# Moving the additions of squared sums from GpSimd to VectorE in a state-space mixer

## The chip, the cores and the metric

The kernel runs on one core of a Trainium2 chip. The metric is the device time of one execution in microseconds (us). The core has a matrix engine (TensorE, PE in the rows; its weight loads are PEld), a vector engine (VectorE, DVE), an engine for functions (ScalarE, ACT), a general one (GpSimd, POOL) and a queue engine (SyncE, SP). Each engine takes its instructions in the order of its own queue and waits on semaphores of the others.

## The reference, cut to what matters

Two layers process 512 prompt positions and 8 samples together. Layer 0 mixes by sparse attention, layer 1 by a state-space (Mamba-2) mixer; each is followed by an MLP. Two norms matter here: the one on the mixer's inner output `y`, and the one on the residual stream ahead of the MLP of layer 1.

```python
def rmsnorm(x, w):
    xf = x.astype(jnp.float32)
    r = lax.rsqrt(jnp.mean(xf * xf, axis=-1, keepdims=True) + EPS)
    return (xf * r).astype(x.dtype) * w
...
def ssd_mixer(h, conv_buf, ssm_state, w_in, conv_w, conv_b, dt_bias, a_log, d_skip, norm_w, w_out):
...
    y = y.astype(h.dtype).reshape(B, T, SSD_D_INNER)
    y = rmsnorm(y * jax.nn.silu(z), norm_w)
    new_state = final.reshape(B, SSD_HEADS, SSD_HEAD_DIM, SSD_STATE).astype(ssm_state.dtype)
    return y @ w_out, new_conv, new_state
...
        xp = xp + mp[2] * op
        xs = xs + ms[2] * os_
        hp = modulate(xp, norm_w[i, 1], mp[3], mp[4])
        hs = modulate(xs, norm_w[i, 1], ms[3], ms[4])
```

## The kernel before, in words

Activations lie with channels on the 128 partitions and the 520 positions (512 prompt, 8 sample) along the free axis. The residual stream is `X`, 8 such tiles; the mixer's inner output is 16 tiles, numbered q. A norm needs the sum of squares over channels: each tile is squared on ACT, the squares of the tiles are added into one tile, and a product with a column of ones on PE sums over the partitions (`rnorm`). A norm can take several tiles, `parts`, one product after the other.

In the state-space stage a loop over q runs `ssd_x` (input product and convolution), `ssd_pair` (two heads: matrices `M`, states `st`, sample states `ss` with `xb`, and `xd` for the products) and `ssd_gate`. `ssd_gate` multiplies `y` by its gate, squares it on ACT into `z`, adds `z` to `yss` at line 1604 on POOL for q of 1 to 14 (q 0 makes `yss`, q 15 is kept in `ysq`), and splits the scaled `y` into a high and a low half, `yh`, on ACT and DVE. All weights are split in the same way (`wh`, ACT line 330 and DVE line 336), since each product is made of three in reduced precision.

After the last tile the output product runs in four groups. In the last, `ssd_out(3, ...)`, each of 8 residual tiles n is finished by `out_add` (line 1631, reads PSUM) and `out_fin` (line 1633): scale `acc`, add to `X` (`c` in the rows), the sample part through a small `t`, then `square` and `scaled` (`us`, and a copy on ACT). `square` gets POOL as its engine there, so that tiles 1 to 6 are added to `ssq` at line 534 on POOL; tile 7 goes to `parts`. In this stage `ssq` lies in a buffer of `st`, and the squares in the two buffers of `M`, which is how the rows call them. `boundary` then makes the norm: products on `st` (that is, `ssq`) and on `M` (tile 7), root, reciprocal, and the modulated input of the MLP. Before it and between, PE has a small product for the conditioning (`ada`).

Elsewhere (`start`, `nsa_out`, `mlp`, `last`) `square` is called without an engine and adds on DVE at line 336.

The order of each queue isn't the order of the code: a scheduler lays the instructions out by priority and planned times, and then sets the semaphores. Buffers of a name rotate; an instruction that writes one waits for the last reader.

Of the kernel before, what the change touches and what calls it, by code (L numbers as in the profile page):

```python
# [14 lines left out]
ALU = mybir.AluOpType  # L15
# [190 lines left out]
BOTH = (0, 1)  # L206


def cols(hs=BOTH):
    return slice(PART[hs[0]][0], PART[hs[-1]][1])  # L210


def prompt(ap, hs=BOTH):
    return two(ap[:, 0:512])[:, hs[0]:hs[-1] + 1]
# [6 lines left out]
def span(ps):  # L221

    return ps.rearrange("p h n -> p (h n)")[:, HP:HP + T]
# [38 lines left out]
class Step:  # L262
# [252 lines left out]
        w = self.nw[:, 2 * l + which, :]  # L515
        self.stt(self.a, self.m[l][:, o + 8:o + 16, :], 1.0, w[:, :, None].to_broadcast([128, 8, 9]), ALU.add, ALU.mult)

    def square(self, k, eng=None, hs=BOTH):
        at = cols(hs)
        x = self.X[:, k, at]  # L520
        if k == 0:
            self.ssq = self.U('ssq')
            self.parts = [self.ssq]
            self.act(self.ssq[:, at], x, AF.Square)

            self.act(self.small([128, 1], 'warm', 2), self.ssq[:, 0:1], AF.Sqrt)
        else:
            s = self.U('sq')
            q = self.ssq[:, at]
            self.act(s[:, at], x, AF.Square)  # L530
            if not eng:
                self.tt(q, q, s[:, at], ALU.add)
            elif k < 7:
                eng.tensor_tensor(self.ssq, self.ssq, s, op=ALU.add)
            else:
                self.parts.append(s)

    def scaled(self, k):
        x = self.X[:, k, :]
# [1049 lines left out]
    def ssd_gate(self, g, t, y):  # L1589

        q = 4 * g + t
        ps = self.product(('w_ssd', 10 * g + 3 + 2 * t), self.h)
        z = self.U('z')
        v = span(ps)
        self.act(z, v, AF.Tanh, scale=0.5)
        self.stt(z, z, 1.0, v, ALU.add, ALU.mult)
        self.tt(y, y, z, ALU.mult)
        if q == 0:
            self.yss = self.U('yss')
            self.act(self.yss, y, AF.Square)  # L1600
        else:
            self.act(z, y, AF.Square)
            if q < 15:
                self.nc.gpsimd.tensor_tensor(self.yss, self.yss, z, op=ALU.add)
            else:
                self.ysq = z
        hi, lo = self.U('yh', F32R), self.U('yh', F32R)
        w = self.snw[:, q:q + 1]
        self.act(hi, y, AF.Copy, scale=w)
        self.stt(lo, y, w, hi, ALU.mult, ALU.subtract)  # L1610
        self.yh[q] = (hi, lo)
# [21 lines left out]
    def out_fin(self, n):  # L1633
        a = self.acc.pop(n)
        self.tt(a, a, self.ry, ALU.mult)
        g = self.m[1][:, 16 + n, :]
        x = self.X[:, n, :]
        self.stt(prompt(x), prompt(a), g[:, 0:1], prompt(x), ALU.mult, ALU.add)
        t = self.small([128, 8], 't8')
        self.tt(t, a[:, 512:T], g[:, 1:9], ALU.mult)  # L1640
        self.tt(x[:, 512:T], x[:, 512:T], t, ALU.add)
        self.square(n, self.nc.gpsimd)
        self.scaled(n)

    def ssd(self, h):
# [326 lines left out]
```

## Time and profile before

| What | us |
|---|---|
| Median of 3 runs | 1719.15 |
| Lowest and highest | 1718.74, 1723.88 |
| Profiled execution | 1717.8 |
| Its span, first to last instruction | 1716.0 |
| PE busy | 1658.1 |
| DVE busy | 983.5 |
| ACT busy | 761.8 |
| POOL busy | 146.4 |

Times in the rows count from the start of the span. A row of a group gives line, engine, operation, names as out<-in, shape and count, then busy time and mean ns of one, then the idle time ahead of it and what ended it. A row of the order of time gives start and duration in us, engine, line, operation and names; in brackets stands the idle time just before. The end of one instruction can lie a little after the start of the next on the same engine.

### The profile page before, as it was taken

The page shows a single profiled execution, that of the slowest core. Times are in us where ns is not written, and L with a number is a line of the kernel's source. Part 1 is how long each engine was busy: PE and PEld are TensorE (multiplying, and loading weights), DVE is VectorE, ACT ScalarE, POOL GpSimd, SP SyncE. Part 2 cuts the span into 40 slices and gives each one's busy share as a digit, 9 for nine tenths or more (in the row PEclk, how much of TensorE's full clock was granted, in tenths as well). Part 3 has the DMA queues.
Part 4 walks back from the last instruction along what each step waited for, and adds up shares of the span by engine and source line. Part 5 has one row for each costly group of instructions (what it writes and reads, how often), then busy time and mean ns, then how long its engine had stood idle before and what let it go on. Part 6 is the DMA issues. An engine that isn't in the chain of part 4 may idle for free.

```text
span 1716.0 us, 34647 instructions
## 1 busy us (share of the span) xinstructions
PE 1658.1 (97%) x13846; PEld 1542.4 (90%) x13846; DVE 983.5 (57%) x2422; ACT 761.8 (44%) x1624; POOL 146.4 (9%) x304
## 2 busy tenths in 40 slices
PE   7999999999999999999999999999998999999997
PEld 6799867667989999999989998999997999999997
DVE  2543377776464343433469968879797643434344
ACT  3534366666443132322456666646564422323231
POOL 1000113310001000000001112111022000000000
PEclk9999999999999999999999999999999999999999
DMA  8823656545433534234433352343324232323221
GB/s 300 290 87 98 215 193 227 166 150 198 135 115 108 175 96 136 88 136 136 137 133 113 132 171 86 119 137 135 129 89 160 75 98 87 99 87 97 88 87 51
DMA packets 72114, 229.87 MB, mean 134 GB/s; under 512 B 8770, under 2 KB 15218, under 8 KB 71186
## 3 DMA queue, kind: packets, MB, share of 16 engines
q1 hardware_dynamic: 62546, 198.45, 35.2%
q0 software_dynamic: 8832, 28.16, 4.6%
q8 instruction: 109, 1.79, 0.4%
q10 hardware_dynamic: 576, 1.05, 0.2%
q14 instruction: 51, 0.42, 0.1%
HBM read 204.02 MB, written 23.61 MB: 133 GB/s over the span
## 4 chain that ended last, share of the span: by engine, by line
PE 69%; DVE 7%; ACT 2%; issue 2%; SPq 1%; POOLq 1%; DMA 0%; POOL 0%; DVEq 0%; ACTq 0%
PE a L323 59%; PE s L323 4%; PE f L323 2%; PE o L323 1%; DVE wh L336 1%; PE sc L323 1%; PE t L327 1%; DVE c L345 1%; ACT wh L330 1%; DVE g L345 1%; PE s L327 1%; DVE acc L336 1%; DVE ss L1465 0%; SPq L395 0%; SPq L393 0%
## 5 line engine op out<-in xcount | busy, mean ns | idle before, releaser
L323 PE MATMUL a<-h,wh 128*128 128x256 f32 x5952 | 743.3, 284 | 4.5 <-ACT t L333 1.6
L323 PEld LDWEIGHTS a<-h,wh 128*128 128x128 f32 x5952 | 723.6, 189 | 10.9 <-issue 3.3
L330 ACT ACTIVATE wh<-w 128x1024 fp32r<-128x1024 f32 x212 | 224.6, 1059 | 522.2 <-PE a L323 479.1
L336 DVE TENSOR_TENSOR wh<-w,wh 128x1024 fp32r<-128x1024 f32 x212 | 259.6, 1225 | 269.4 <-ACT wh L330 268.8
L323 PEld LDWEIGHTS a<-hid,wh 128*128 128x128 f32 x3072 | 370.2, 188 | 5.0 <-issue 4.2
L323 PE MATMUL a<-hid,wh 128*128 128x256 f32 (+1 forms) x3072 | 373.6, 283 | 0.0
L336 DVE TENSOR_TENSOR t<-a,c 128x8 f32<-128x8 f32 x72 | 12.0, 167 | 216.1 <-PE a L323 216.1
L323 PE MATMUL a<-yh,wh 128*128 128x256 f32 (+1 forms) x768 | 99.7, 288 | 3.4 <-DVE acc L336 1.9
L323 PEld LDWEIGHTS a<-yh,wh 128*128 128x128 f32 x768 | 95.0, 191 | 5.6 <-DVE acc L336 2.6
L330 ACT ACTIVATE hid<-t 128x520 fp32r<-128x520 f32 x64 | 40.8, 639 | 84.5 <-DVE t L336 84.5
L330 ACT ACTIVATE h<-t 128x128 f32<-128x128 f32 (+3 forms) x128 | 52.8, 441 | 51.5 <-PE t L327 50.8
L333 ACT ACTIVATE h<-sc,m 128x128 f32<-128x128 f32 (+3 forms) x128 | 66.6, 529 | 10.4 <-DVE m L340 7.4
L336 DVE TENSOR_TENSOR hid<-t,hid 128x520 fp32r<-128x520 f32 x64 | 44.7, 700 | 42.3 <-ACT hid L330 42.3
L345 DVE SCALAR_TENSOR_TENSOR c<-a,c,c 128x512 f32<-128x512 f32 (+1 forms) x74 | 53.9, 728 | 1.8 <-PE a L323 1.8
L327 PE MATMUL t<-c,h 128*128 128x128 f32 x320 | 53.7, 281 | 1.1 <-DVE h L340 0.7
L333 ACT ACTIVATE xb<-bc,x 128x128 f32<-128x128 f32 x128 | 46.4, 419 | 15.6 <-DVE xb L345 11.1
L327 PEld LDWEIGHTS t<-c,h 128*128 128x128 f32 x320 | 35.1, 141 | 14.0 <-issue 8.8
L323 PEld LDWEIGHTS a<-q,wh 128*128 128x128 f32 x384 | 46.3, 188 | 1.0 <-ACT wh L330 0.8
L323 PE MATMUL sc<-kv,q 128*128 128x128 f32 (+3 forms) x128 | 47.1, 380 | 0.0
L323 PE MATMUL a<-q,wh 128*128 128x256 f32 (+1 forms) x384 | 46.7, 283 | 0.0
L323 PE MATMUL sc<-kv,c 128*128 128x128 f32 (+3 forms) x128 | 41.8, 338 | 4.3 <-POOL c L947 4.3
L1465 DVE SCALAR_TENSOR_TENSOR ss<-ss,c,xb 128x128 f32<-128x128 f32 x128 | 43.5, 363 | 3.9 <-ACT xb L333 3.6
(367 smaller groups left out, 1935.9 us busy)
## 6 DMA issues: line engine op xcount, KB each, us to landing
w<-in_w_dram SPq DMA_DIRECT2D x128, 512.0 KB, 3.5
w<-in_ada_w_dram SPq DMA_DIRECT2D x80, 512.0 KB, 3.6
w<-in_w_ssd_dram SPq DMA_DIRECT2D x40, 512.0 KB, 3.6
w<-in_w_nsa_dram SPq DMA_DIRECT2D x20, 512.0 KB, 3.8
ss<-in_ssm_dram SPq DMA_DIRECT2D x16, 512.0 KB, 4.3
out_ssm_s_dram<-ss POOLq DMA_DIRECT2D x16, 512.0 KB, 3.2
w<-in_w_sout_dram SPq DMA_DIRECT2D x16, 512.0 KB, 3.8
cm<-in_cmp_dram SPq DMA_DIRECT2D x24, 256.0 KB, 5.1
```

The lines of the kernel that those rows point to most:

```text
L323: self.nc.tensor.matmul(out, lhsT, rhs, start=start, stop=stop, skip_group_check=True)
L327: self.nc.tensor.transpose(out, in_, self.C('ident')[0:k, 0:k])
L330: self.nc.scalar.activation(out, in_, AF.Copy, **kw)
L333: self.nc.scalar.activation(out, in_, f, **kw)
L336: self.nc.vector.tensor_tensor(out, a, b, op=op)
L345: self.nc.vector.scalar_tensor_tensor(out, a, s, b, op0=op0, op1=op1, **kw)
L1465: self.nc.vector.scalar_tensor_tensor(out, a, s, b, op0=op0, op1=op1)
```

## The change

`square` loses its parameter for an engine and gets `apart`: a tile's squares either go to `parts` or are added on DVE. `out_fin` asks for `apart` at tile 7 alone. In `ssd_gate` the addition to `yss` is made on DVE.

```diff
-    def square(self, k, eng=None, hs=BOTH):
+    def square(self, k, apart=False, hs=BOTH):
...
             self.act(s[:, at], x, AF.Square)
-            if not eng:
+            if apart:
+                self.parts.append(s)
+            else:
                 self.tt(q, q, s[:, at], ALU.add)
-            elif k < 7:
-                eng.tensor_tensor(self.ssq, self.ssq, s, op=ALU.add)
-            else:
-                self.parts.append(s)
...
             self.act(z, y, AF.Square)
             if q < 15:
-                self.nc.gpsimd.tensor_tensor(self.yss, self.yss, z, op=ALU.add)
+                self.tt(self.yss, self.yss, z, ALU.add)
             else:
                 self.ysq = z
...
-        self.square(n, self.nc.gpsimd)
+        self.square(n, n == 7)
         self.scaled(n)
```

## Rows read from the trace of the kernel before

**Rows 1.** The page, first part: busy us (share of the span) and instructions
```profile
PE 1658.1 (97%) x13846; PEld 1542.4 (90%) x13846; DVE 983.5 (57%) x2422; ACT 761.8 (44%) x1624; POOL 146.4 (9%) x304
```
**Rows 2.** Stretches: length, busy PE, PEld, DVE, ACT, POOL, clock, DMA share, GB/s
```profile
930.00:1300.00 370.00, 362.18 (x2955) 343.78 (x2954) 309.23 (x874) 226.45 (x582) 58.60 (x99) 1.00 0.39 130
...
1318.00:1325.00 7.00, 2.73 (x19) 0.60 (x11) 6.93 (x16) 2.99 (x5) 3.42 (x2) 1.00 0.90 328
1325.00:1334.00 9.00, 7.79 (x38) 6.89 (x37) 3.96 (x10) 3.92 (x8) 0.00 (x0) 0.62 0.23 84
...
484.00:490.00 6.00, 6.00 (x30) 5.84 (x31) 6.00 (x15) 3.60 (x10) 0.00 (x0) 0.56 0.10 40
```
**Rows 3.** Who PE waited for, 930 to 1350: us in total, times, longest
```profile
PE s L323 <- DVE xd L336: 3.9, 5, 0.8
PE s L323 <- POOL st L534: 3.9, 1, 3.9
```
**Rows 4.** Groups of instructions on POOL
```profile
L1604 POOL TENSOR_TENSOR yss<-yss,z 128x520 f32<-128x520 f32 x14 | 18.7, 1335 | 90.7 <-ACT z L333 90.7
...
L534 POOL TENSOR_TENSOR st<-st,M 128x520 f32<-128x520 f32 x6 | 9.0, 1494 | 27.3 <-ACT M L333 27.3
```
**Rows 5.** POOL, ACT and PE in order of time, an earlier boundary and this one
```profile
479.35 1.28 PE L323 MATMUL t<-c,ssq 128*128 128x1 f32 x10 [0.60 <-DVE ssq L336]
...
1322.99 1.71 POOL L534 TENSOR_TENSOR st<-st,M 128x520 f32<-128x520 f32 x1 [1.58 <-ACT M L333]
1324.75 1.65 PE L323 MATMUL s<-c,st 128*128 128x1 f32 x10 [3.86 <-POOL st L534]
1325.02 0.64 ACT L333 ACTIVATE M<-c 128x520 f32<-128x520 f32 x1 [1.07 <-DVE c L336]
1326.25 2.27 PE L323 MATMUL s<-c,M 128*128 128x1 f32 x10
```
**Rows 6.** DVE in order of time at the boundary: start, us, instruction
```profile
1305.22 1.81 DVE L345 SCALAR_TENSOR_TENSOR c<-acc,c,c 128x512 f32<-128x512 f32 x1
...
1308.86 1.27 DVE L336 TENSOR_TENSOR us<-c,A 128x8 f32<-128x8 f32 x1
1310.05 0.74 DVE L345 SCALAR_TENSOR_TENSOR c<-acc,c,c 128x512 f32<-128x512 f32 x1
...
1310.79 0.68 DVE L336 TENSOR_TENSOR acc<-acc,a 128x520 f32<-128x520 f32 x1
1311.40 0.15 DVE L336 TENSOR_TENSOR c<-c,t 128x8 f32<-128x8 f32 x1
...
1312.81 1.49 DVE L345 SCALAR_TENSOR_TENSOR c<-acc,c,c 128x512 f32<-128x512 f32 x1
...
1323.47 1.25 DVE L336 TENSOR_TENSOR t<-acc,c 128x8 f32<-128x8 f32 x1
```
**Rows 7.** Groups on DVE by form, 440 to 500, the attention's output stage
```profile
L336 DVE TENSOR_TENSOR ssq<-ssq,sq 128x520 f32<-128x520 f32 x7 | 4.9, 696 | 0.6 <-ACT sq L333 0.6
```
**Rows 8.** DVE in order of time beside additions of `yss` on POOL
```profile
951.44 1.80 DVE L345 SCALAR_TENSOR_TENSOR x<-cv,c,x 128x512 f32<-128x512 f32 x1
...
1049.24 0.61 DVE L1465 SCALAR_TENSOR_TENSOR ss<-ss,c,xb 128x128 f32<-128x128 f32 x2
1049.76 0.29 DVE L345 SCALAR_TENSOR_TENSOR xb<-ss,bc 128x128 f32<-128x128 f32 x1
...
1049.97 1.40 DVE L345 SCALAR_TENSOR_TENSOR xb<-ss,bc 128x128 f32<-128x128 f32 x1
...
1098.50 1.30 DVE L345 SCALAR_TENSOR_TENSOR yh<-y,c,yh 128x520 fp32r<-128x520 f32 x1 [1.33 <-ACT yh L333]
...
1173.90 1.48 DVE L1465 SCALAR_TENSOR_TENSOR ss<-ss,c,xb 128x128 f32<-128x128 f32 x2
...
1278.79 1.58 DVE L1465 SCALAR_TENSOR_TENSOR ss<-ss,c,xb 128x128 f32<-128x128 f32 x2
```
**Rows 9.** The chain that ended last, 1170 to 1182: start, us, what
```profile
1173.98 1.40 DVE ss L1465 x2
```

## The prediction

> **What bounds the kernel now.** I read the page's first part, then the stretches by engine, then who waited for whom, and last the order of time on single engines. The page gives TensorE 97% of the span, VectorE (DVE) 57%, GpSimd (POOL) 9% [rows 1]. That average hides two stages. In the state-space stage, 930 to 1300 us, PE is busy 362.18 of 370 us and DVE 309.23 [rows 2]: PE sets the pace, and DVE, at 84%, is late here and there. At the boundary after it, 1318 to 1325 us, PE is busy only 2.73 of 7 us while DVE is busy 6.93 [rows 2]: there DVE sets the time. The waits agree: PE waits 3.9 us once for POOL's `st`, the last addition at line 534, and 3.9 us in five pieces for DVE's `xd` [rows 3]. The additions to be moved are two groups on POOL: 14 of `yss` at 1335 ns and 6 of `st` at 1494 ns [rows 4].
>
> What matters most is next to these additions. While POOL adds, one DVE instruction beside it is stretched. At the boundary, POOL's last addition runs from 1322.99 to 1324.70 [rows 5]; DVE's `t`, 128x8, begins at 1323.47 and takes 1.25 us, ending at 1324.72, where an addition of the same shape takes 0.15 [rows 6]. I went through all 20 additions and found one such stretched instruction beside each. So POOL's additions are not free for DVE: it loses about 1 us to most of them, more than an addition on DVE itself takes, 0.696 us in an earlier stage with the same shape [rows 7].
>
> **The change part by part.** "The last tile's squares kept apart" is nothing new: before, too, tile 7 goes into `self.parts` and q 15 into `ysq`. What changes is the engine of 6 + 14 additions. No DMA is moved; POOL only loses work, and what stands behind these additions on it (casts, copies, stores) can only come earlier. I set that at nothing.
>
> *Price of one addition on DVE.* The busy time is 0.70 us, but the next instruction begins 0.61 us after such a 520-column addition begins, as 1310.79 to 1311.40 shows [rows 6]. I take 0.61; the upper end is 0.70.
>
> *Boundary, 6 additions.* DVE has no gap from 1304 to 1324.7, so every microsecond in its queue counts. The stretches are: `c` 1.81 against 0.74, or 1.07; `us`, 128x8, 1.27 against 0.15, or 1.12, twice; `c` 1.49, or 0.75; `t` 1.25 against 0.15, or 1.10, twice [rows 6]. Sum 1.07 + 1.12 + 1.12 + 0.75 + 1.10 + 1.10 = 6.26 us taken away. Added: 6 x 0.61 = 3.66. Net 2.60. Then the end of the chain: the Square of tile 7 on ACT starts at 1325.02 and takes 0.64; its product with ones starts at 1326.25, behind the 10 products on `st` from 1324.75, which take 1.65 [rows 5]. With the addition of tile 6 ended before the Square of tile 7, those 10 products no longer stand in the way, which could give up to 0.5 more; put late in DVE's order, it gives back some 0.2. I take 2.6, with 2.4 to 3.1 as the ends while DVE doesn't wait.
>
> *The added wait.* The addition must wait for ACT's Square. Behind it on DVE stand, at the boundary, the next tile's scaling and the small `us`; in the state-space stage the low half of `yh`, the state updates and the weight splits, and PE waits for some of these. The order in the trace isn't the code's: DVE takes up tile n+1's `acc` before tile n's last small addition, so other work is there to stand between. I take a wait of nothing; the upper end is the whole Square, 0.64 plus about 0.1 of signalling, 0.75 us each.
>
> *State-space stage, 14 additions.* Each frees what its stretched neighbour lost, less 0.61. It counts only where PE then waits for DVE. Three of the five waits for `xd` follow a stretched `xb`, 1.40 against 0.29 in the one shown [rows 8]: 1.11 - 0.61 = 0.50. Two follow a stretched `yh`, 1.30 against 0.75 as its neighbours, 0.55 [rows 8]; there DVE was idle until ACT had written the high half (1.33 us of idleness stand before the row), and the addition falls into that gap, so that also about 0.50 comes free. Each wait is 0.7 to 0.8 us long, so 0.50 fits in: 5 x 0.50 = 2.5. Three more stretched instructions lie on the chain that ended last: `x` at 951, 1.80 against 0.74, frees 0.45; `ss` x2 at 1173, 1.48 against 0.61, frees 0.26, and the chain shows it with 1.40; `ss` x2 at 1278, 1.58, frees 0.36 [rows 8, 9]. Sum 2.5 + 1.07 = 3.6. The other six stand beside unbroken PE work and give nothing. Lower end 0, if PE hides all of it; upper end 14 x 0.5 = 7.0.
>
> *Clock.* After PE's idleness before 1324.75 the granted clock falls: 0.62 on average from 1325 to 1334, that is between the levels 2.4 and 1.2 GHz, after 1.00 [rows 2]. The 10 products on `M` take 2.27 us there; 10 of the same shape took 1.28 at an earlier boundary, after 0.60 us of idleness [rows 5]. A shorter gap might keep the clock up. The 10 products that follow those on `M` are as many, so the bound is 2 x (2.27 - 1.28) = 2.0 us. But an earlier boundary also shows 0.56 from 484 to 490 us [rows 2]; a fallen clock is common at these places. I take 0 and keep 2.0 for the range.
>
> *Sum.* 2.6 + 3.6 = 6.2 us. The profiled execution has 1717.8 us (span 1716.0 and 1.8 around it), so 1711.6 after. It lies 1.35 under the median of the three runs, 1719.15; made against that median, the forecast is 1713.0 us, 0.36% faster. About 0.3% (5.2 us) is what a measurement of this kernel can tell from no change.
>
> **The rivals.**
> *PE hides the state-space part.* For it: PE is busy 98% of that stage. Against: the five waits for `xd`. Only the boundary pays: 1719.15 - 2.6 = 1716.5, no difference that can be told.
> *The clock stays up as well.* 6.2 + 2.0 = 8.2: 1711.0.
> *DVE waits for the Square.* The place is DVE's queue in both stages: if the new order puts each addition directly behind what feeds its Square, it costs 0.75 + 0.61 = 1.36 us instead of the stretch, and from a wait of about 0.43 us (1.04 - 0.61) on the change loses. Boundary: 6 x 1.36 - 6.26 = +1.9. State-space stage: about 0.3 more at each of the six places on the path where DVE had other work, +1.8, less 1.0 at the two where it was idle. Together +2.7: 1721.9, slower than before, if under what can be told. Against it: work of the next tile is at hand to stand between.
> *The stretches are not POOL's and stay.* Then the additions come on top of a full DVE: 6 x 0.61 at the boundary and 0.61 at each of the six busy places on the path, 7.3 us: 1726.5. Against it: 20 of 20 stretches beside POOL's additions. The Trainium skill, "Perfetto Trace Analysis", section "Optimizing Scalar/DVE Operations", says that with a saturated DVE offloading work, even to GpSimd, may make sense, which speaks against this change; it adds that the two share a port, so that this might not help. The rows here follow the second half.
> *The order is dealt anew and it comes to nothing.* About 1719, since the order of all queues follows from the planned times, and those of PE may shift by a few tenths at many places.
>
> **How the numbers follow.** Forecast 0.42 (1711 to 1716), PE hides it 0.22, clock stays up 0.16, dealt anew 0.08, DVE waits 0.05, stretches stay 0.07. Over 0.3% faster: 0.30 of the forecast's 0.42 and the clock's 0.16, together 0.46. Slower by over 0.3%: the stretches' 0.07, 0.02 of the waiting case, where ACT comes to its Square later than shown, and 0.02 of the order dealt anew: 0.11. Within: 0.43. The range: its lower end takes in the clock and the upper bound of the state-space stage (7.0 + 2.6 + 2.0 = 11.6, that is 1707.6, all of it at once); its upper end takes in the boundary alone, the order dealt anew and half of the waiting case (half of 2.7 over 1719.15): 1707.6 to 1720.5.
>
> **What would show it.** Right: no line-534 or line-1604 instruction on POOL; 20 more DVE additions of 520 columns at 0.70 us; mean `yh` at line 345 and `c` there near 0.75; no 1.25 us `t` or `us`; PE's wait before the `st` products down from 3.9 to 2 us or less; the five waits for `xd` near 0.3. Wrong: DVE idle before the additions for ACT's Square, stretched instructions with no POOL addition beside them, or PE's idleness in 930 to 1300 unchanged.

## The result, and the profile after

The changed kernel takes 1709.52 us in the median (22 runs), the kernel before 1719.53 us beside it (22 runs). The ratio is 0.9942, with a 95% interval from 0.9924 to 0.9960: 10.0 us faster, between 6.9 and 13.1. The forecast was 6.2 us. The profiled execution took 1709.68 us, with a span of 1708.0 us.

The page of the changed kernel, first part: each engine's busy us, share of the span and instructions.

```profile
PE 1661.1 (97%) x13846; PEld 1544.8 (90%) x13846; DVE 978.6 (57%) x2442; ACT 762.3 (45%) x1624; POOL 117.9 (7%) x284
```

Against [rows 1], 20 instructions went from POOL to DVE. DVE is busy 4.9 us less although it does 20 instructions more: its neighbours of POOL's additions had lost more than the 20 additions take. The groups of the changed kernel on DVE in the state-space stage and the boundary, 870 to 1325 us (busy us, mean ns | idle time before them), show the same:

```profile
L345 DVE SCALAR_TENSOR_TENSOR yh<-y,c,yh 128x520 fp32r<-128x520 f32 x16 | 12.1, 756 | 1.3 <-ACT yh L333 1.3
L336 DVE TENSOR_TENSOR yss<-yss,z 128x520 f32<-128x520 f32 x14 | 9.7, 696 | 4.5 <-ACT z L333 4.5
```

The additions cost 696 ns as in [rows 7], and `yh` is at 756 ns; the 1.30 of [rows 8] is gone. At the boundary, DVE in order of time (start, us, instruction):

```profile
1297.55 0.69 DVE L336 TENSOR_TENSOR st<-st,M 128x520 f32<-128x520 f32 x1
1298.16 0.75 DVE L345 SCALAR_TENSOR_TENSOR c<-acc,c,c 128x512 f32<-128x512 f32 x1
1298.82 0.16 DVE L336 TENSOR_TENSOR t<-acc,c 128x8 f32<-128x8 f32 x1
...
1314.08 0.70 DVE L336 TENSOR_TENSOR st<-st,M 128x520 f32<-128x520 f32 x1
```

The next instruction begins 0.61 us after an addition begins, `c` takes 0.75 and `t` 0.16, where [rows 6] has 1.81, 1.49 and 1.25. What PE waited for in the changed kernel, 930 to 1340 us (us in total, times, longest):

```profile
PE s L323 <- DVE st L336: 2.0, 1, 2.0
PE a L323 <- DVE c L348: 1.4, 1, 1.4
PE s L323 <- DMA w<-in_ada_w_dram: 0.8, 1, 0.8
...
PE a L323 <- DVE acc L336: 0.3, 1, 0.3
```

Against [rows 3], the wait before the products on `st` fell from 3.9 to 2.0 us, and the five waits for `xd` (3.9 us) are gone altogether; a wait for `c` at line 348 has come.

**Where the time went.** I cut each trace at the same instructions: the first `yh` on ACT (the state-space stage begins), the first product `s<-c,z` on PE (it ends), the first product on `M` (boundary), the first of the second half's MLP, and the first of its second matrix. Each length is the difference of two starts in one trace, in us; the last two lines are the us at half clock (1.2 instead of 2.4 GHz), from the trace's clock records.

| | before | before again (e11) | after | after again (e3) |
|---|---|---|---|---|
| state-space stage | 357.97 | 357.93 | 351.34 | 351.37 |
| to the product on `M` | 33.55 | 33.90 | 30.67 | 31.24 |
| to the MLP | 6.46 | 6.46 | 6.46 | 6.46 |
| MLP, first matrix | 59.58 | 61.46 | 61.61 | 61.19 |
| half clock, up to `M` | 4.17 | 4.97 | 1.21 | 2.20 |
| half clock, `M` to second matrix | 6.07 | 12.10 | 12.44 | 11.45 |

Everything between there and the last norm takes 307.94 us in both kernels. In the profiled pair the span falls by 8.0 us: 6.63 in the state-space stage and 2.88 to the product on `M`, less 2.03 that the MLP gives back, and 0.5 more at places that the change doesn't touch. Single executions spread by more than the gain for reasons ahead of these stages: one of 1721.02 us (e2) reached the first `yh` at 945.04 us with 44.4 us at half clock before it, that of the kernel before at 934.74 us with 17.1. The sections below ask three things: whether it is POOL's reading that stretches DVE, why the state-space stage gives 6.6 us where 3.6 was forecast, and whether what the MLP gives back belongs to the change.

### The profile page after: what moved, and what is told of

It reads as the page before. It is cut to its first block, busy times and chain, and to the rows that moved or that the text cites. A ratio compares the mean times of both kernels' runs of the same rounds, so it can differ in the third digit from the quotient of the medians.

```text
span 1708.0 us, 34635 instructions
## 1 busy us (share of the span) xinstructions
PE 1661.1 (97%) x13846; PEld 1544.8 (90%) x13846; DVE 978.6 (57%) x2442; ACT 762.3 (45%) x1624; POOL 117.9 (7%) x284
## 4 chain that ended last, share of the span: by engine, by line
PE 76%; DVE 2%; issue 1%; ACT 1%; SPq 1%; POOLq 0%; DMA 0%; POOL 0%; DVEq 0%; ACTq 0%
PE a L323 64%; PE s L323 5%; PE f L323 2%; PE o L323 1%; PE sc L323 1%; PE t L327 1%; PE s L327 1%; DVE c L345 0%; SPq L395 0%; SPq L393 0%; POOLq L393 0%; PE f L327 0%; DVE g L345 0%; DMA w<-in_selk_dram 0%; DVE wh L336 0%
## 5 line engine op out<-in xcount | busy, mean ns | idle before, releaser
L323 PEld LDWEIGHTS a<-h,wh 128*128 128x128 f32 x5952 | 726.9, 190 | 13.1 <-issue 3.8
L340 DVE TENSOR_SCALAR h<-h,z 128x128 f32<-128x128 f32 (+3 forms) x128 | 44.4, 384 | 1.3
```

The source lines that it names most:

```text
L323: self.nc.tensor.matmul(out, lhsT, rhs, start=start, stop=stop, skip_group_check=True)
L340: self.nc.vector.tensor_scalar(out, a, s1, None, op0=op0)
```

## The experiments

Diffs are against the changed kernel, ratios against the kernel before, measured beside each run. Theory: POOL's additions stretch DVE, and PE waits for the stretched work. First rival: the stretches aren't POOL's. Second: the gain is that of a new order of the queues.

**One half of the change at a time.** e1 puts the additions of `yss` back on POOL:

```
-                self.tt(self.yss, self.yss, z, ALU.add)
+                self.nc.gpsimd.tensor_tensor(self.yss, self.yss, z, op=ALU.add)
```

> Only the six additions at the boundary go to DVE, the fourteen of yss stay on POOL. PE's order differs from that of the kernel before in three lines only. If the stretches of DVE beside POOL's additions are what is given back, the boundary gains its 2.9 us (measured between the two traces) and nothing else changes: 0.9983 of before. If the gain came from a new order of PE's queue, this kernel gains nothing: 1.000.

Measured: ratio 1.0003 [0.9982, 1.0023]. The state-space stage is 357.94 us, as before; the boundary 32.29, 1.3 to 1.6 us less; the MLP's first matrix 60.96. PE's wait before the products on `st` is 1.96 us, as in the changed kernel.

e2 puts the six of `ssq` back on POOL:

```
+            elif mixer:
+                self.nc.gpsimd.tensor_tensor(self.ssq, self.ssq, s, op=ALU.add)
...
-        self.square(n, n == 7)
+        self.square(n, n == 7, mixer=True)
```

> Only the fourteen additions of yss go to DVE. If the state-space stage gives its 6.6 us and the boundary is a separate account, 0.9962 of before. The order of PE is that of the changed kernel, so a new order and freed stretches can't be told apart here; e4 and e6 do that. If the two parts were not additive (one moving the other's wait), less than 3 us.

Measured: 0.9979 [0.9959, 0.9999]; state-space stage 351.34 us, boundary 33.35. By the trace, the gates' additions bring their whole 6.6 us here, the larger part of the change's gain; the interval left room, so it was measured once more (e12, below).

e3 is the changed kernel beside them:

> The changed kernel once more, beside the others on this chip: 0.9942 of before, and the sum of e1 and e2 if the parts are additive.

Measured: 0.9932 [0.9909, 0.9956], stages as in the table. That the two parts add up doesn't show in the times: e1 and e2 come to 0.0018 together, e3 has 0.0068. It shows in the stages: 6.6 and 1.3 to 1.6 us against 8.9 to 9.8 for both, as far as the clock lets it be told.

**Is it POOL's reading?** e6 is the changed kernel, in which POOL also adds each of the 20 squares into a tile that nothing reads. The instructions of PE, DVE and ACT stand in the order of the changed kernel.

```
+                self.nc.gpsimd.tensor_tensor(self.other, self.other, s, op=ALU.add)
...
+                self.nc.gpsimd.tensor_tensor(self.other, self.other, z, op=ALU.add)
```

> The changed kernel, and POOL besides adds every square into a tile that nobody reads: the stretches come back, in exactly the changed kernel's order of PE, DVE and ACT. If POOL's additions are what stretches DVE: 6 us more at the boundary, 5 to 8 us more in the state-space stage, so 1.000 to 1.003 of before. If the new order made the gain: it stays, 0.995 to 0.997.

Measured: 1.0028 [0.9999, 1.0056], 1726.59 us; the state-space stage takes 361.19 us, 9.85 more than in the changed kernel and above the 5 to 8 expected, the boundary 36.45, 5.2 to 5.8 more, of which a part may be the clock (6.8 us at half clock there against 1.2 and 2.2). The same two groups on DVE as above, in e6, 930 to 1300 us:

```profile
L345 DVE SCALAR_TENSOR_TENSOR yh<-y,c,yh 128x520 fp32r<-128x520 f32 x16 | 19.3, 1209 | 1.3 <-ACT yh L333 1.3
L336 DVE TENSOR_TENSOR yss<-yss,z 128x520 f32<-128x520 f32 x14 | 16.6, 1186 | 4.5 <-ACT z L333 4.5
...
L345 DVE SCALAR_TENSOR_TENSOR z<-z,a 128x520 f32<-128x520 f32 x16 | 11.0, 689 | 1.5 <-ACT z L333 1.5
```

With nothing else changed, the two groups that stand beside POOL's additions grow from 756 to 1209 and from 696 to 1186 ns in the mean (single ones take 1.8 us, others their old time); `z`, elsewhere in the order, stays at 689. So the first rival falls.

e4 lets POOL write instead of read: it fills each square with zeros, twice. These 20 squares don't enter the sums.

```
+                for _ in range(2):
+                    self.nc.gpsimd.memset(s, 0.0)
...
-                self.tt(self.yss, self.yss, z, ALU.add)
+                for _ in range(2):
+                    self.nc.gpsimd.memset(z, 0.0)
```

> In place of each of the twenty additions POOL fills the tile of squares with zeros, twice, when the square is there: the sums are left out, POOL is as busy at the same places, but it writes only and reads nothing. DVE gets no additions, and PE's and DVE's order are nearly those of the kernel before. If it is POOL's reading that stretches DVE: no stretched instruction beside these, yh at 0.75 us, and more gained than by the change itself, 6.3 us at the boundary and 6 to 8 us in the state-space stage, 0.991 to 0.993. If any POOL instruction beside DVE does it: as before, 0.998 to 1.000. If the gain of the change came from the new order: near 1.000 as well, but without stretches.

e5 leaves the same 20 additions out and puts nothing in their place:

> All twenty additions are left out, on both engines; the squares stay. PE's order is nearly that of the kernel before. This is the bound: what the additions cost in all. If DVE's lateness is the cost, 6.3 us at the boundary and some 7 us in the state-space stage: 0.991 to 0.993 of before, some 3 us under the changed kernel. If the changed kernel's gain came mostly from its new order of PE's queue: no better than the changed kernel, 0.994 to 0.997.

Measured: e4 0.9918 [0.9893, 0.9942], e5 0.9914 [0.9886, 0.9942]; state-space stage 353.48 and 353.50 us, boundary 26.45 and 26.35. The ratios are as expected, the stage is not: it falls by 4.5 us in both, where some 7 were expected. The boundary falls by 7.1 to 7.6 us instead of 6.3, but is also without the half clock that before has there. POOL's zeros, and `yh` beside them, in e4:

```profile
L1606 POOL MEMSET z<- 128x520 f32 x28 | 14.9, 533 | 90.7 <-ACT z L333 89.9
...
L345 DVE SCALAR_TENSOR_TENSOR yh<-y,c,yh 128x520 fp32r<-128x520 f32 x16 | 12.1, 757 | 8.7 <-ACT yh L333 8.7
```

Twenty-eight instructions of 533 ns on POOL cost nothing against e5, and `yh` stays at 757 ns, though a write overlaps the `yh` in 13 of 14 tiles; beside none of e4's 40 writes is a DVE instruction over 0.1 us longer than in e5. So neither POOL's being busy nor its writing stretches DVE; of what an addition does, its reading is left. No run lets POOL read without writing. The Trainium skill, "SBUF — State Buffer", section "Who interferes with whom", says that a DVE instruction with two inputs in SBUF contends with a GpSimd instruction that reads SBUF, not with one that only writes it; e6 and e4 agree, 1209 against 757 ns.

**Why 6.6 us and not 3.6.** e5 has no additions at all, and its state-space stage is still 2.16 us longer than that of the changed kernel, which has 14 more on DVE. The instructions stand in another order: comparing PE's list of this stage line by line, by the names and shapes in the traces, e5 differs from the kernel before in 58 lines, the changed kernel in 398. Two kernels set the order apart from the cost. In e10, DVE writes zeros into each square instead of adding it (these 14 squares don't enter the gates' sum); PE's instructions stand exactly as in the changed kernel.

```
-                self.tt(self.yss, self.yss, z, ALU.add)
+                self.nc.vector.memset(z, 0.0)
```

> The changed kernel, in which VectorE writes zeros into each square of the gates instead of adding it (the gates' sum of squares is left out). TensorE's instructions stand in exactly the order of the changed kernel, and VectorE reads nothing for the sum. Theory (the order carries the rest of the gain, and the addition's own time on VectorE is hidden): the state-space stage takes 351.3 us as in the changed kernel, some 2.1 us under the run with all additions left out in the old order (353.50). Rival (the order is worth nothing): 353 us or so, as with all additions left out; or well under 351 us if VectorE's additions had cost time in the changed kernel.

In e9, DVE adds and then also writes zeros (read by nothing), with which the order goes part of the way back: by the same count 248 lines from the kernel before and 370 from the changed kernel.

```
                 self.tt(self.yss, self.yss, z, ALU.add)
+                self.nc.vector.memset(z, 0.0)
```

> The changed kernel, in which VectorE also writes zeros into each square of the gates after adding it (the square is read by nothing afterwards). The additions stay on VectorE, but with the longer work behind each gate the planner lays TensorE's instructions of the state-space stage nearly in the order of the kernel before (990 lines differ from it, 2,446 from the changed kernel, 2,620 between those two). Theory (part of the state-space gain comes from the new order of TensorE's instructions): the stage from the first yh to the first product with z takes 353.5 us or more, as with the additions left out in the old order, against 351.34 in the changed kernel, and the ratio is about 0.9955. Rival (the gain comes from the work taken from GpSimd alone, and the order is worth nothing): 351.3 to 351.8 us, ratio about 0.994.

Measured: e10 0.9926 [0.9898, 0.9953], e9 0.9983 [0.9954, 1.0011], with 0.9955 expected; its interval takes in 1. The stage by windows (stretch, length, busy PE, PEld, DVE, ACT, POOL, clock, DMA share, GB/s): before, e5 (no additions, order near before), e9 (additions and zeros, an order between), e10 (zeros, new order), after (additions, new order).

```profile
934.74:1292.71 357.97, 350.15 (x2871) 332.19 (x2870) 300.68 (x853) 218.86 (x570) 56.58 (x96) 1.00 0.38 126
```
```profile
937.25:1290.74 353.49, 349.34 (x2870) 332.08 (x2870) 290.30 (x853) 216.96 (x570) 38.89 (x82) 1.00 0.38 128
```
```profile
943.95:1299.78 355.83, 349.79 (x2870) 333.25 (x2869) 303.19 (x881) 219.44 (x570) 32.26 (x82) 1.00 0.38 128
```
```profile
936.33:1287.64 351.31, 349.50 (x2871) 332.18 (x2870) 296.40 (x867) 218.63 (x568) 36.22 (x82) 1.00 0.38 128
```
```profile
934.54:1285.88 351.34, 349.49 (x2870) 332.11 (x2869) 298.63 (x867) 218.79 (x568) 37.78 (x82) 1.00 0.38 128
```

Read length less busy PE, PE's idleness: 7.82 before, 4.15 in e5, 6.04 in e9, 1.81 in e10, 1.85 after. DVE's busy time doesn't rank them: the changed kernel has 8.3 us more of it than e5 and is the shorter. In one and the same order, an addition of 696 ns and a write of 492 ns give the same stage (351.34, 351.31): what an addition takes beyond a write costs nothing there. Neither e5 nor e9 comes under 353.49 us. e9 isn't a clean copy of the old order with the additions alone, for it has 6.9 us of writing more and 3.4 us at half clock; it only shows that the additions on DVE don't bring the 6.6 us by themselves. What e5 and e10 show is that the order is worth at least about 2.2 us: e10 is the shorter one with 14 instructions more on DVE.

One place shows how. Before, between `yh` and `xd` on DVE, stands a weight split `wh`, and PE waits for `xd`; in e5 too. Before and e5, in order of time:

```profile
1101.31 1.22 DVE L336 TENSOR_TENSOR wh<-w,wh 128x1024 fp32r<-128x1024 f32 x1
...
1102.53 0.68 DVE L336 TENSOR_TENSOR xd<-s,c 128x512 f32<-128x512 f32 x1
...
1103.36 1.13 PE L323 MATMUL s<-xd,g 128*128 128x128 f32 x8 [0.81 <-DVE xd L336]
```
```profile
1102.27 1.30 DVE L336 TENSOR_TENSOR wh<-w,wh 128x1024 fp32r<-128x1024 f32 x1
...
1103.57 0.67 DVE L336 TENSOR_TENSOR xd<-s,c 128x512 f32<-128x512 f32 x1
...
1104.39 1.13 PE L323 MATMUL s<-xd,g 128*128 128x128 f32 x8 [0.29 <-DVE xd L336]
```

The changed kernel at the same place:

```profile
1095.74 0.70 DVE L336 TENSOR_TENSOR yss<-yss,z 128x520 f32<-128x520 f32 x1 [0.71 <-ACT z L333]
1096.36 0.76 DVE L345 SCALAR_TENSOR_TENSOR yh<-y,c,yh 128x520 fp32r<-128x520 f32 x1
...
1099.14 0.67 DVE L336 TENSOR_TENSOR xd<-s,c 128x512 f32<-128x512 f32 x1
...
1100.10 1.16 PE L323 MATMUL s<-xd,g 128*128 128x128 f32 x8
```

From the start of `yh` to that of `xd` it is 4.03 us before, 3.53 in e5 (the stretch of 0.54 gone, the split still there) and 2.78 after: no split stands between them, and PE doesn't wait. The planner, which now counts work of DVE's for each gate (a write in its place, e10, gives PE the same order), put the split elsewhere. I found this twice, before `xd` at 1102.53 and at 1207.32; at the other places the order changed in other ways, and I didn't trace each. The largest piece is elsewhere: two waits of PE for `acc`, 1.9 us, stand before and in e5 and are gone in the changed kernel.

**Does the clock take the boundary's gain?** In the changed kernel the granted clock is 0.88 from 1310 to 1317 us and 0.50, the lower level, from 1316.56 up to the MLP. e7 keeps PE busy with 25 products that nothing reads:

```
+            self.fill(dummy, 22)
...
+            self.fill(dummy, 1, True)
...
+            self.fill(dummy, 2, True)
```

> The changed kernel with 22 products of constants on PE ahead of the products with ones at the boundary, 1 behind them and 2 behind the broadcast of the root; nobody reads what they write. The granted clock stood at half for 13.65 us after this boundary in the changed kernel's trace, which I put at 4 to 5 us. If PE's idleness of 0.8 and 2.0 us there is what lets the clock fall: 1.00 from the boundary on and 2 to 4 us under the changed kernel, 0.992 of before. If the low activity of the norm's own small products does it: the clock falls all the same, and the time is that of the changed kernel or up to 1 us more.

Measured: 0.9932 [0.9904, 0.9961]. The half clock is 0 up to `M` and 6.83 us behind, and the MLP's first matrix takes 59.62 us; but from `M` to the MLP it takes 7.61 us instead of 6.46. From the product with `z` to the second matrix: 98.61 us against 98.74 and 98.89. The fillers cost what the clock gives.

e8 keeps tile 6 apart as well, so that one addition less stands late in DVE's queue:

```
-        self.square(n, n == 7)
+        self.square(n, n >= 6)
```

> The changed kernel with tile 6 kept apart as well as tile 7, and a third product with ones: one addition of 0.61 us less in DVE's full queue at the boundary, and PE's 10 products on the sum no longer wait for it. 0.6 to 1.0 us under the changed kernel, which the runs can hardly tell; the trace should show the first products with ones some 2 us earlier.

Measured: 0.9925 [0.9900, 0.9949], the same stretch 98.34 us: not to be told from the changed kernel. The first products with ones do come earlier, 3.9 us against the 2 expected, and what follows gives it back. No version that makes all the sums beats the changed kernel clearly.

By then the MLP's first matrix had taken 59.58 us in the profile of before and 59.62 in e2, and 60.6 to 61.7 in nearly all others, and I took the loss for a cost of the change. Two more runs test that, the kernel before (e11) and e2's kernel (e12; its expectation says seven additions, they are fourteen):

> The kernel before once more, for its stages. If the longer stretch at half clock behind the boundary (10 to 13.7 us in every profile without GpSimd's additions of ssq, 6.1 in the profile of before) belongs to the change, this one shows about 6 us again, and 59.6 us from the first product of the second half's MLP to the first of its second matrix; if it is chance, it may show 10 us and 61 us. The state-space stage should be 358.0 us again.

> The seven additions of the state-space stage on VectorE, the boundary as in the kernel before, once more. The stage should take 351.3 us against 358.0, so a ratio of 0.9961 by the trace; the first measurement gave 0.9979, with an interval up to 0.9999. A ratio under 0.9985 with an interval clear of 1 goes with the trace. For the clock behind the boundary: three profiles with GpSimd's additions of ssq have shown 59.58, 59.62 and 61.46 us from the first product of the second half's MLP to the first of its second matrix, nine without them 60.6 to 61.7. Above 60.5 us here says that the longer stretch at half clock comes with either boundary; 59.6 us leaves a leaning towards the change.

Measured: 61.46 us in e11 and 61.76 in e12. The windows of that stretch, in the kernel before, e11 and the changed kernel:

```profile
1332.72:1392.30 59.58, 58.38 (x481) 57.77 (x481) 32.98 (x52) 25.57 (x42) 0.00 (x0) 1.00 0.30 88
```
```profile
1329.35:1390.81 61.46, 60.68 (x481) 60.05 (x481) 32.99 (x52) 25.56 (x42) 0.00 (x0) 0.95 0.27 85
```
```profile
1323.02:1384.62 61.60, 60.82 (x480) 60.20 (x481) 32.97 (x52) 25.57 (x42) 0.00 (x0) 0.95 0.24 78
```

The kernel before has the same 0.95 and the same 2 us more in its second profile. So the 2.03 us of the profiled pair aren't a cost that the change must have. With POOL's additions of `ssq` in place, two profiles of four (before, e2, e11, e12) had the short stretch; with DVE adding `ssq`, or nothing adding it, and no fillers, none of nine (e6, where POOL adds besides, among them). A leaning towards the long one may be left; so few profiles don't settle it. e12's ratio is 0.9951 [0.9927, 0.9975] with the stage at 351.30 us: clear of 1, and around the 0.9961 that 6.6 us make.

## Why the prediction was right, and where it was short

*What bounds the kernel; the stretched neighbours* [rows 2 to 6, 8]: right. PE waits for DVE, and DVE is slowed while POOL adds; e6 brings the stretches back in an unchanged order, e4 shows that POOL busy with writes does nothing.

*Price of an addition*, 0.61 to 0.70 us: right, 0.61 from start to start and 0.70 busy.

*Boundary*, 2.6 us: right in kind, somewhat too high. The mean over four profiles with POOL's additions there is 33.54 us (33.55, 33.90, 33.35, 33.34), over the five with the changed boundary (after, e3, e10, e1, e9) 31.43 (30.67, 31.24, 31.25, 32.29, 31.72): 2.1 us. Part of that may be the clock: the first four have 4.3 us at half clock in the stretch, the five 3.4; the difference can be worth 0.5 at most, if work takes twice as long there. So DVE's queue gives 1.6 to 2.1. Up to the second matrix, with the clock behind, the same profiles have 100.60 and 99.15 us: 1.4 us. The two terms hold within wide bounds: against e4 and e5, 26.4 us with no half clock, POOL's additions cost 5.0 to 7.1 (6.26 in the prediction), DVE's 3.4 to 5.0 (3.66), the lower ends less half of the time at half clock. e1, which does this part alone, shows no gain in its time, but 2.6 us (ratio 0.9985) lies in its interval. The last addition and the Square of tile 7 stood late: PE began the products on `M` at 1316.56, right behind those on `st`, so that the further 0.5 us of the prediction wasn't to be had.

*Added wait*, nothing: about right, but not because other work stands between. DVE does wait for ACT's Square, at 7 places, in the changed kernel, which the prediction had named as a sign of being wrong (waits on DVE, 930 to 1340 us):

```profile
DVE yss L336 <- ACT z L333: 4.5, 7, 0.7
```

That is the rival's mechanism, 0.64 us on average, and longer than its break-even of 0.43 us. But it lies where DVE was idle before, as the prediction had it for two places: DVE's waits for `yh` on ACT were 9.6 us in the kernel before and 8.7 in e4, and are 1.3 now, as the groups show. Additions and waits together can cost the stage no more than the idleness that PE has left there, 1.85 us, of which 1.4 are a wait for DVE's `c`.

*State-space stage*, 3.6 us within 0 to 7.0: the term that was too small; it measured 6.63 (e12: 6.67 against 357.97). The step that failed is that the order stays, on which the sum over the old places rests. PE's idleness falls by 3.67 us in e5, which looks like the 3.6, but by coincidence: e5 has no additions on DVE either, and without their 0.61 each the prediction's own terms come to 6.3 (the three waits behind `xb` whole, 2.3; two of 0.55 behind `yh`; 1.06, 0.87 and 0.97 on the chain). Place by place, the two waits behind `yh`, forecast at about 0.3, are 0.29 and 0.28 in e5, and the three behind `xb` are gone. Of the three places on the chain only `x` at 951 shows a wait of PE's, 1.0 for `xs`, gone in e5; behind the two stretched `ss`, PE has no wait for DVE over 0.2 us even before. And e5 has new waits for `c` and `g`, 0.9 us together. So in the old order, additions on DVE could hardly have given more than the 3.67 of idleness; no run has them there. Who PE waited for in the kernel before, 934 to 1288 us, beside the waits for `xd` [rows 3]:

```profile
PE a L323 <- DVE acc L336: 1.9, 2, 1.0
PE s L323 <- DVE xs L345: 1.0, 1, 1.0
PE s L323 <- DVE g L1465: 0.4, 2, 0.3
```

And in e5, the same stretch:

```profile
PE a L323 <- DVE acc L336: 1.9, 2, 1.0
PE s L323 <- DVE g L1465: 0.9, 3, 0.4
PE s L323 <- DVE xd L336: 0.6, 2, 0.3
PE a L323 <- DVE c L348: 0.6, 1, 0.6
```

The changed kernel has none of these waits but that for `c`, 1.4 us. The rival "the order is dealt anew" named the right mechanism and took it to come to nothing: it is worth at least 2.30 us of idleness (4.15 to 1.85). The rest, 0.66 us (350.15 to 349.49), is PE's own busy time, which falls by 0.81 in e5; why, I can't say.

*Clock*, nothing, with up to 2.0 us of gain: about right. It differs by 2 us between profiles of one kernel, in either direction. The rival in which it stays up is out: all 6.46 us from the products on `M` to the MLP are at half clock, in the profile of before 6.07 of them. That PE hides the state-space part, and that the stretches stay, are both out too.

*The sum*: 6.63 and 1.4 to 2.1 make 8.0 to 8.7 us, against the 10.0 measured [6.9 to 13.1] and the 6.2 forecast. What the forecast lacks is in the state-space term, and most of that is the order. That the time still lies in the range is partly luck: the lower end was built from 14 additions that each free 0.5 us and from a clock that stays up, and the measured gain beyond the forecast comes from neither.

## What to carry to other kernels

Before counting work on GpSimd as free, look at the VectorE instruction beside each of its reading instructions: if these lose in sum more than the operations would take on VectorE itself, try moving the operations, even onto a VectorE that is 84% busy. Where a planner deals the queues from planned times, moving an operation changes the order of everything behind it; leave the operation out in the old order and replace it in the new one, and the two stages give a lower bound for what the order is worth. And before charging a loss of 2 us at a lower clock to a change, profile the kernel before a second time.

## What the hardware showed beyond that

The stretch goes both ways: beside DVE's additions, POOL's takes 1576 and 1775 ns in e6, where [rows 4] has 1335 and 1494. Which instruction is stretched follows one pattern in the kernel before: at all 20 additions it is the first one on DVE with two tiles as inputs that begins after POOL's has begun, and it ends 0.55 to 0.56 us after POOL's with 512 or 520 columns, 0.15 with 128 and 0.02 to 0.03 with 8; one that is already running keeps its time. In e6, in order of time:

```profile
1036.79 0.70 DVE L336 TENSOR_TENSOR yss<-yss,z 128x520 f32<-128x520 f32 x1 [0.71 <-ACT z L333]
1036.85 1.81 POOL L1608 TENSOR_TENSOR c<-c,z 128x520 f32<-128x520 f32 x1 [16.05 <-ACT z L333]
1037.41 1.80 DVE L345 SCALAR_TENSOR_TENSOR yh<-y,c,yh 128x520 fp32r<-128x520 f32 x1
```

The granted clock behind the boundary is not a property of the kernel: the kernel before had 6.07 us at half clock there in one profile and 12.10 in the next.
